# Whole products for the first pair of gate and up blocks, and three pieces of down kept behind the last block product

## The chip, the cores and the metric

The kernel runs on one core of a Trainium2 chip. The metric is the device time of one execution in microseconds (us). The core's engines work side by side, each through its own queue in order: TensorE (PE, matrix products), VectorE (DVE), ScalarE (ACT), GpSimd (POOL) and SyncE (SP, which issues most DMAs). They wait for one another by semaphores.

## What is computed

Two blocks in float32, one after the other. The first has two layers of attention. The second puts 16 meta tokens ahead of 512 rows, and goes through an even mixer, a convolutional feed-forward, an odd mixer, a second feed-forward and a last norm. The change lies in the two feed-forwards:

```python
def conv_ffn(h, w_up, w_gate, conv_w, conv_b, w_down):
    u = h @ w_up
    g = h @ w_gate
    g = lax.conv_general_dilated(g, conv_w[:, None, :].astype(g.dtype), window_strides=(1,),
                                 padding=[(CONV_WIDTH - 1, 0)],
                                 dimension_numbers=('NWC', 'WIO', 'NWC'),
                                 feature_group_count=D_FF) + conv_b
    return (jax.nn.silu(g) * u) @ w_down
...
        h = h + conv_ffn(rmsnorm(h, norm_ffn[l]), ffn_w_up[l], ffn_w_gate[l],
                         ffn_conv_w[l], ffn_conv_b[l], ffn_w_down[l])
    return rmsnorm(h, norm_final)[:, N_META:N_META + S]
```

The model is 1024 wide, the feed-forward 2816, the convolution 3 rows long.

## The kernel before

The residual X lies in SBUF transposed: 8 row blocks of 128 features, 528 columns of tokens (the second feed-forward uses 516 of them for gate and up and 512 for down). A float32 product is made of three products of rounded parts: each operand is split into a high part (ACT, a copy) and a low part (DVE, the difference), and the matmuls are high x high, high x low, low x high. `weights` (lines 149 to 165) loads a weight tile of 128 x 1024 by SP's queue into `wr` and splits it into `wh` and `wl`; `split` (lines 169 and 170) does the same for anything else; `dense` (line 179) issues matmuls.

A feed-forward has 22 blocks of 128 for gate and for up, taken in 11 pairs: i and i + 11. `paired` makes both blocks of a pair of one matrix by seven products of quarters in place of eight (lines 1204 to 1257): four sums of weight quarters (`ws`, line 1216), lows of 1024 columns of the raw weights (`wl`), of the sums (`wl`, `wx`) and one of 512 (`wy`), and then 7 products x 4 row blocks x 3 parts = 84 matmuls of 264 columns (258 in the second feed-forward; line 1240), in the banks `ps_a` and `ps_mm`. Copies by ACT (lines 1244, 1247, 1250) and sums by DVE (1251, 1256) put the result together. The right operands of the seven are made by `seven` (lines 1155 to 1202) from X and the norm's gain: the parts of two quarters (1172, 1173, 1182, 1183), sums of quarters t1 to t4 (1180, 1186 to 1188) and their splits, with the square sums of the norm (246, 249, 256) beside them. The norm's factor `rs` is taken into gate and up only behind the products; it comes by ones matmuls (256), ACT (226), POOL (227), transposes by PE (273) and an ACT copy (1201).

For each pair: gate, its product by rs (1136 to 1138), the convolution (1084 by ACT, two steps of 1086 by DVE), silu (1087, ACT), once more times rs (1088, POOL), up, the product of both (1142 to 1144), and a split into `aH` and `aL` (7 buffers each). The products by down are 8 pieces for each group of pairs (`after`; the groups are cut at 0, 1, 3, 5, 7, 9, 11): a piece adds one row block of X (1113). `between` puts pieces of the group before into places between the products of a pair. In the first feed-forward the last group's pieces follow at the end; in the second, `final` does the last group by halves of columns together with the last norm (lines 1259 to 1284).

Ahead of each feed-forward a mixer ends with products by its output weights (yH and yL are its operands, line 179), and DVE adds each to X (line 708). The order of all instructions on each engine is set by the language's scheduler, which goes by its own costs and by the buffers that come free.

Of the kernel before, what the change touches and what calls it, by code (L numbers as in the profile page):

```python
# [9 lines left out]
F32 = mybir.dt.float32  # L10
F32R = mybir.dt.float32r
AF = mybir.ActivationFunctionType
# [18 lines left out]
def two(x):  # L31

    return x.rearrange("p (a b) -> p a b", a=2)
# [29 lines left out]
class Norm:  # L63
# [35 lines left out]
    def done(self):  # L99
        rs = self.net.row_tile("rs", self.w)  # L100
        for out, a, b in self.net.rstd(self.pp, self.sums, 1.0 / D):
            self.net.nc.scalar.activation(rs[:, a:b], out, AF.Copy)
        return self.h, rs


class Net:
# [958 lines left out]
    def ffn(self, l, out=None):  # L1065
# [6 lines left out]
        with ExitStack() as c:  # L1072
# [2 lines left out]
            new = lambda name, cols, bufs, dt=F32: fp.tile([128, cols], dt, name=name, tag=name, bufs=bufs)  # L1075
            cw = fp.tile([128, 22, 4], F32, name="cw")
            nc.gpsimd.dma_start(cw, d[f"conv_{l}"])
            ops, rs = self.seven(pp, fp, X, self.gain[:, 6 + l])
            act, units = ([], []), []

            def activated(i, g):
# [32 lines left out]

                return [lambda o=o: unit(o) for o in range(8)]

            slots = 0

            def between():

                nonlocal slots
                for _ in range(-(-len(units) // max(slots, 1))):
                    units.pop(0)()
                slots -= 1

            cuts = (0, 1, 3, 5, 7, 9, 11)
            for a, b in zip(cuts, cuts[1:]):
                slots = 4 * (b - a)
                for i in range(a, b):
                    g = [new("g", lead + n, 3) for _ in range(2)]  # L1130
                    if u == 0:
                        for t in g:
                            nc.vector.memset(t[:, :2], 0.0)
                    e = g[0][:, lead - u:]
                    f, t = self.paired(pp, fp, d[f"gate_{l}"], i, ops, e, m, between)
                    nc.vector.tensor_tensor(e, e, rs, op=OP.mult)  # L1136
# [9 lines left out]
                        done(t)  # L1146
                if out is None or b < 11:
                    units += after(a, b)
            if out is None:
                for unit in units:  # L1150
                    unit()
            else:
                self.final(pp, fp, d[f"down_{l}"], act, 2 * a, 2 * b, out)

    def seven(self, pp, fp, x, g):

        nc, w = self.nc, x.shape[2]
        m = w // 2  # L1160
        ng = fp.tile([128, 8], F32, name="ng")
        nc.vector.tensor_scalar(ng, g, -1.0, None, op0=OP.mult)
        free = [self.hp.tile([128, T2], F32R, name="h", tag="h", bufs=16)[:, :w] for _ in range(16)]
        more = lambda: free.pop() if free else fp.tile([128, T2], F32R, name="op", tag="op", bufs=12)[:, :w]
        first = [[more() for _ in range(2)] for _ in range(2)]
        sums = self.sums(pp, w, 8)
        ops = [([], []) for _ in range(4)]
        for k in range(4):
            j = k + 4
            x1, x2, gk, gj = x[:, k], x[:, j], g[:, k:k + 1], g[:, j:j + 1]  # L1170
            h, l = (first[i][k // 2][:, m * (k % 2):m * (k % 2) + m] for i in range(2))
            nc.scalar.activation(h, x1[:, :m], AF.Copy, scale=gk)
            nc.vector.scalar_tensor_tensor(l, x1[:, :m], gk, h.bitcast(F32), op0=OP.mult, op1=OP.subtract)
            ops[0][0].append(h)
            ops[0][1].append(l)
            b12 = fp.tile([128, T2], F32, name="z", tag="z", bufs=4)[:, :m]
            nc.scalar.activation(b12, x1[:, m:], AF.Copy, scale=gk)
            s = [fp.tile([128, T2], F32, name="g", tag="g", bufs=3)[:, :w] for _ in range(2)]
            t1, t2, t3, t4 = s[0][:, :m], s[0][:, m:], s[1][:, :m], s[1][:, m:]
            nc.vector.scalar_tensor_tensor(t1, x1[:, :m], gk, b12, op0=OP.mult, op1=OP.subtract)  # L1180
            h, l = more(), more()
            nc.scalar.activation(h, x2, AF.Copy, scale=gj)
            nc.vector.scalar_tensor_tensor(l, x2, gj, h.bitcast(F32), op0=OP.mult, op1=OP.subtract)
            ops[1][0].append(h)
            ops[1][1].append(l)
            nc.vector.scalar_tensor_tensor(t2, x2[:, m:], ng[:, j:j + 1], t1, op0=OP.mult, op1=OP.subtract)
            nc.vector.scalar_tensor_tensor(t3, x2[:, m:], gj, b12, op0=OP.mult, op1=OP.subtract)
            nc.vector.scalar_tensor_tensor(t4, x2[:, :m], ng[:, j:j + 1], t2, op0=OP.mult, op1=OP.subtract)
            for i in range(2):
                h, l = more(), more()  # L1190
                self.split(h, l, s[i])
                ops[2 + i][0].append(h)
                ops[2 + i][1].append(l)
            sums(x1)
            sums(x2)
        lo, hi = slice(0, m), slice(m, w)
        cols = lambda i, c: [[t[:, c] for t in part] for part in ops[i]]
        right = {1: ops[0], 2: cols(1, lo), 3: cols(1, hi), 5: cols(2, lo), 6: cols(2, hi), 7: cols(3, lo), 4: cols(3, hi)}
        rs = self.row_tile("rs", w)
        for out, a, b in self.rstd(pp, sums, 1.0 / D):  # L1200
            nc.scalar.activation(rs[:, a:b], out, AF.Copy)
        return right, rs

    def paired(self, pp, fp, src, i, right, e, m, between):

# [196 lines left out]
```

## Time and profile before

| | us |
|---|---|
| median of 3 runs (lowest, highest) | 2141.17 (2140.36, 2142.55) |
| the profiled execution | 2140.01 |
| its span in the trace | 2138.3 |
| PE, DVE, ACT, POOL busy | 2034.8, 1518.1, 980.4, 570.6 |

Busy time is the sum of an engine's instructions in the span. The timeline gives for each instruction its start, its length, engine, line, operation, output and inputs, and in brackets the idle time ahead of it with what ended that. Neighbouring instructions overlap in it, so the price of one in a row of many is the step from one start to the next. A window gives the busy time of each engine in a stretch, the clock granted to PE (1.00 is 2.4 GHz, 0.50 is 1.2 GHz) and the DMA traffic.

### The profile page before, as it was taken

How to read it: one execution, taken by the hardware profiler on the slowest of the kernel's cores; microseconds unless marked ns; L12 is line 12 of the kernel's file. 1: busy time of each engine (PE TensorE's matmuls, PEld its weight loads, DVE VectorE, ACT ScalarE, POOL GpSimd, SP SyncE). 2: the span in 40 equal slices, each digit the busy share in tenths (PEclk: the TensorE clock that was granted, in tenths of full speed). 3: DMA queues.
4: the chain of work that ended last, by engine and by line, in shares of the span. 5: the costliest groups of instructions: out<-in, count | busy, mean ns of one | idle time of the engine just before them, and what ended most of it. 6: DMA issues, size and time to landing. Idle time of an engine off the chain costs nothing. (4 is left out here: it accounts for less than half of the span.)

```text
span 2138.3 us, 36583 instructions
## 1 busy us (share of the span) xinstructions
PE 2034.8 (95%) x14384; PEld 1863.6 (87%) x14384; DVE 1518.1 (71%) x2506; ACT 980.4 (46%) x1783; POOL 570.6 (27%) x652
## 2 busy tenths in 40 slices
PE   8999999999989999999989999999989988999997
PEld 6788888788889889988979999999878988889997
DVE  5565756665676896555788888875645788988885
ACT  5455645455644322344445444444334454544444
POOL 2322223222235555363001101103435401011011
PEclk9999999999999999999989999999989989999998
DMA  6643224533224322442222333324333222233222
GB/s 198 185 108 102 65 91 134 163 103 101 64 72 120 89 89 89 125 135 67 95 69 89 99 99 99 99 90 130 92 89 106 71 95 89 90 104 100 92 85 64
DMA packets 81163, 216.53 MB, mean 101 GB/s; under 512 B 10872, under 2 KB 16528, under 8 KB 80992
## 3 DMA queue, kind: packets, MB, share of 16 engines
q1 hardware_dynamic: 77360, 205.93, 32.2%
q0 software_dynamic: 2336, 7.19, 1.2%
q8 instruction: 113, 1.85, 0.4%
q10 hardware_dynamic: 1296, 1.09, 0.2%
q14 instruction: 58, 0.48, 0.1%
HBM read 166.20 MB, written 6.92 MB: 81 GB/s over the span
## 5 line engine op out<-in xcount | busy, mean ns | idle before, releaser
L179 PE MATMUL ps_mm<-hH,wh 128*128 128x264 f32 (+3 forms) x1480 | 393.1, 322 | 18.4 <-ACT hH L82 6.9
L179 PE MATMUL ps_mm<-hL,wh 128*128 128x264 f32 (+3 forms) x1480 | 395.1, 320 | 11.4 <-DVE hL L83 11.4
L179 PE MATMUL ps_mm<-hH,wl 128*128 128x264 f32 (+3 forms) x1480 | 393.6, 319 | 0.0
L163 ACT ACTIVATE wh<-wr 128x1024 fp32r<-128x1024 f32 (+3 forms) x213 | 209.4, 984 | 266.4 <-PE ps_mm L179 204.0
L179 PEld LDWEIGHTS ps_mm<-hH,wh 128*128 128x128 f32 (+1 forms) x1480 | 249.4, 191 | 38.6 <-DVE t L203 7.8
L164 DVE TENSOR_TENSOR wl<-wr,wh 128x1024 fp32r<-128x1024 f32 (+3 forms) x189 | 230.8, 1222 | 66.6 <-ACT wh L163 61.6
L179 PEld LDWEIGHTS ps_mm<-hL,wh 128*128 128x128 f32 (+1 forms) x1480 | 250.7, 191 | 29.4 <-DVE hL L83 13.0
L179 PEld LDWEIGHTS ps_mm<-hH,wl 128*128 128x128 f32 (+1 forms) x1480 | 250.8, 191 | 18.0 <-issue 1.4
L1088 POOL TENSOR_TENSOR z<-z,rs 128x528 f32<-128x528 f32 (+1 forms) x44 | 82.9, 1900 | 591.4 <-ACT z L1087 591.4
L179 PE MATMUL ps_mm<-aH,wh 128*128 128x264 f32 (+2 forms) x528 | 139.5, 319 | 6.3 <-ACT aH L169 4.1
L179 PE MATMUL ps_mm<-aL,wh 128*128 128x264 f32 (+2 forms) x528 | 138.6, 317 | 0.8 <-DVE aL L170 0.8
L179 PE MATMUL ps_mm<-aH,wl 128*128 128x264 f32 (+2 forms) x528 | 135.3, 316 | 0.1
L203 DVE TENSOR_TENSOR t<-ps_mm,rs 128x528 f32<-128x528 f32 (+1 forms) x101 | 70.2, 696 | 88.6 <-PE ps_mm L179 83.1
L1240 PE MATMUL ps_a<-h,wh 128*128 128x264 f32 (+1 forms) x528 | 103.1, 288 | 9.3 <-DVE z L1143 4.5
L169 ACT ACTIVATE wh<-ws 128x1024 fp32r<-128x1024 f32 x44 | 46.6, 1059 | 126.3 <-PE ps_mm L179 80.0
L179 PEld LDWEIGHTS ps_mm<-aH,wh 128*128 128x128 f32 x528 | 88.9, 190 | 12.6 <-ACT aH L169 4.3
L179 PE MATMUL ps_mm<-yH,wh 128*128 128x264 f32 (+2 forms) x392 | 95.8, 310 | 0.2 <-DVE X L708 0.2
L179 PE MATMUL ps_mm<-yH,wl 128*128 128x264 f32 (+2 forms) x392 | 95.3, 309 | 0.0
L1240 PEld LDWEIGHTS ps_a<-h,wh 128*128 128x128 f32 x528 | 84.4, 192 | 12.5 <-issue 4.7
L179 PEld LDWEIGHTS ps_mm<-aL,wh 128*128 128x128 f32 x528 | 88.9, 190 | 7.2 <-DVE aL L170 1.7
L179 PE MATMUL ps_mm<-yL,wh 128*128 128x264 f32 (+2 forms) x392 | 94.1, 306 | 0.0
L179 PEld LDWEIGHTS ps_mm<-aH,wl 128*128 128x128 f32 x528 | 88.2, 190 | 5.8 <-DVE wl L164 0.3
(342 smaller groups left out, 5013.9 us busy)
## 6 DMA issues: line engine op xcount, KB each, us to landing
wr<-w1c SPq DMA_DIRECT2D x52, 512.0 KB, 3.9
wr<-gate SPq DMA_DIRECT2D x44, 512.0 KB, 3.2
wr<-up SPq DMA_DIRECT2D x44, 512.0 KB, 3.3
wr<-down SPq DMA_DIRECT2D x40, 512.0 KB, 3.6
ks<-st SPq DMA_DIRECT2D x48, 264.0 KB, 5.0
wr<-we_b SPq DMA_DIRECT2D x24, 512.0 KB, 3.6
wr<-wo_c SPq DMA_DIRECT2D x24, 512.0 KB, 3.8
qs<-st SPq DMA_DIRECT2D x64, 132.0 KB, 3.0
```

The lines of the kernel that those rows point to most:

```text
L163: nc.scalar.activation(high, raw, AF.Copy)
L164: getattr(nc, eng).tensor_tensor(low, raw, high.bitcast(F32), op=OP.subtract)
L169: self.nc.scalar.activation(high, x, AF.Copy)
L179: self.nc.tensor.matmul(p[:a.shape[2]], a[:, k], b[k][:, t], start=bool(first and k == 0 and j == 0), stop=bool(last and k == len(ah) - 1 ...
L203: self.nc.vector.tensor_tensor(f(out), v, f(r), op=OP.mult)
L1088: nc.gpsimd.tensor_tensor(z, z, rs[:, u:], op=OP.mult)
L1240: nc.tensor.matmul(ps, p[:, k], q[k], start=start and k == 0 and v == 0, stop=k == 3 and v == 2, skip_group_check=not start)
```

## The change

Pair 0 of gate and of up is done by whole products: `whole` takes both blocks of the pair through all 8 row blocks, 2 blocks x 8 x 3 parts x 2 halves of columns = 96 matmuls. Their right operands (`plain`) are the parts of X by halves; one quarter that the seven don't need (`b12`) is split into buffers of `aH` and `aL`. The norm and the sums of quarters for the seven now stand behind gate's whole products in the code; the sums use two `ws` buffers in place of three `g`. The loop over pairs begins at 1. In the last group `spare` is 3: three pieces of down aren't put between the products but follow the loop, in the second feed-forward ahead of `final`. The removed body of `seven` stands above.

```diff
--- before.py
+++ after.py
@@ -1075,7 +1075,19 @@
             new = lambda name, cols, bufs, dt=F32: fp.tile([128, cols], dt, name=name, tag=name, bufs=bufs)
             cw = fp.tile([128, 22, 4], F32, name="cw")
             nc.gpsimd.dma_start(cw, d[f"conv_{l}"])
-            ops, rs = self.seven(pp, fp, X, self.gain[:, 6 + l])
+            plain, norm, seven = self.operands(pp, fp, new, X, self.gain[:, 6 + l])
+
+            def whole(src):
+
+                banks = [self.bank(pp, 0, w) for _ in range(2)]
+                W = [self.weights(src[11 * j]) for j in range(2)]
+                for k in range(8):
+                    for (wh, wl), (_, ps, _) in zip(W, banks):
+                        for j, (p, part) in enumerate(((wh, 0), (wh, 1), (wl, 0))):
+                            for h in range(2):
+                                nc.tensor.matmul(ps[h][0], p[:, k], plain[h][part][k], start=k == 0 and j == 0, stop=k == 7 and j == 2)
+                return [v for _, _, v in banks]
+
             act, units = ([], []), []
 
             def activated(i, g):
@@ -1114,23 +1126,44 @@
 
                 return [lambda o=o: unit(o) for o in range(8)]
 
-            slots = 0
+            spare, slots = 0, 0
 
             def between():
 
                 nonlocal slots
-                for _ in range(-(-len(units) // max(slots, 1))):
+                for _ in range(-(-max(len(units) - spare, 0) // max(slots, 1))):
                     units.pop(0)()
                 slots -= 1
 
-            cuts = (0, 1, 3, 5, 7, 9, 11)
+            def gates():
+                g = [new("g", lead + n, 3) for _ in range(2)]
+                if u == 0:
+                    for t in g:
+                        nc.vector.memset(t[:, :2], 0.0)
+                return g
+
+            v = whole(d[f"gate_{l}"])
+            rs = norm()
+            ops = seven()
+            g = gates()
+            for j in range(2):
+                nc.vector.tensor_tensor(two(g[j][:, lead - u:]), v[j], two(rs), op=OP.mult)
+            z = [activated(11 * j, g[j]) for j in range(2)]
+            v = whole(d[f"up_{l}"])
+            for j in range(2):
+                if u == 0:
+                    nc.vector.tensor_tensor(two(z[j]), two(z[j]), v[j], op=OP.mult)
+                else:
+                    nc.vector.tensor_tensor(z[j][:, m - u:], z[j][:, m - u:], v[j][:, 1], op=OP.mult)
+                    nc.vector.tensor_tensor(z[j][:, :m - u], z[j][:, :m - u], v[j][:, 0, u:], op=OP.mult)
+                done(z[j])
+            units += after(0, 1)
+
+            cuts = (1, 3, 5, 7, 9, 11)
             for a, b in zip(cuts, cuts[1:]):
-                slots = 4 * (b - a)
+                slots, spare = 4 * (b - a), 3 if b == 11 else 0
                 for i in range(a, b):
-                    g = [new("g", lead + n, 3) for _ in range(2)]
-                    if u == 0:
-                        for t in g:
-                            nc.vector.memset(t[:, :2], 0.0)
+                    g = gates()
                     e = g[0][:, lead - u:]
                     f, t = self.paired(pp, fp, d[f"gate_{l}"], i, ops, e, m, between)
                     nc.vector.tensor_tensor(e, e, rs, op=OP.mult)
@@ -1146,13 +1179,13 @@
                         done(t)
                 if out is None or b < 11:
                     units += after(a, b)
-            if out is None:
-                for unit in units:
-                    unit()
-            else:
+            for unit in units:
+                unit()
+            if out is not None:
                 self.final(pp, fp, d[f"down_{l}"], act, 2 * a, 2 * b, out)
 
-    def seven(self, pp, fp, x, g):
+    def operands(self, pp, fp, new, x, g):
+
 
 
 
@@ -1165,41 +1198,54 @@
         first = [[more() for _ in range(2)] for _ in range(2)]
         sums = self.sums(pp, w, 8)
         ops = [([], []) for _ in range(4)]
+        b12 = [], []
+
+        def parts(h, l, x, gain):
+            nc.scalar.activation(h, x, AF.Copy, scale=gain)
+            nc.vector.scalar_tensor_tensor(l, x, gain, h.bitcast(F32), op0=OP.mult, op1=OP.subtract)
+            return h, l
+
         for k in range(4):
...
+            pair = tuple(first[i][k // 2][:, m * (k % 2):m * (k % 2) + m] for i in range(2))
+            for out, pair, t, j in ((ops[0], pair, x[:, k, :m], k), (b12, tuple(new(n, S if w < T2 else T2, 7, F32R)[:, :m] for n in ("aH", "aL")), x[:, k, m:], k)):
+                for i, v in enumerate(parts(*pair, t, g[:, j:j + 1])):
+                    out[i].append(v)
+            sums(x[:, k])
+        for k in range(4, 8):
+            for i, v in enumerate(parts(more(), more(), x[:, k], g[:, k:k + 1])):
+                ops[1][i].append(v)
+            sums(x[:, k])
         lo, hi = slice(0, m), slice(m, w)
         cols = lambda i, c: [[t[:, c] for t in part] for part in ops[i]]
-        right = {1: ops[0], 2: cols(1, lo), 3: cols(1, hi), 5: cols(2, lo), 6: cols(2, hi), 7: cols(3, lo), 4: cols(3, hi)}
...
+        join = lambda a, b: [p + q for p, q in zip(a, b)]
+        plain = join(ops[0], cols(1, lo)), join(b12, cols(1, hi))
+
+        def norm():
+            rs = self.row_tile("rs", w)
+            for out, a, b in self.rstd(pp, sums, 1.0 / D):
+                nc.scalar.activation(rs[:, a:b], out, AF.Copy)
+            return rs
+
+        def seven():
+            for k in range(4):
+                j = k + 4
+                x1, x2, gk, gj = x[:, k], x[:, j], g[:, k:k + 1], g[:, j:j + 1]
+                b = fp.tile([128, T2], F32, name="z", tag="z", bufs=4)[:, :m]
+                nc.scalar.activation(b, x1[:, m:], AF.Copy, scale=gk)
+                s = [fp.tile([128, 1024], F32, name="ws", tag="ws", bufs=2)[:, :w] for _ in range(2)]
+                t1, t2, t3, t4 = s[0][:, :m], s[0][:, m:], s[1][:, :m], s[1][:, m:]
+                nc.vector.scalar_tensor_tensor(t1, x1[:, :m], gk, b, op0=OP.mult, op1=OP.subtract)
+                nc.vector.scalar_tensor_tensor(t2, x2[:, m:], ng[:, j:j + 1], t1, op0=OP.mult, op1=OP.subtract)
+                nc.vector.scalar_tensor_tensor(t3, x2[:, m:], gj, b, op0=OP.mult, op1=OP.subtract)
+                nc.vector.scalar_tensor_tensor(t4, x2[:, :m], ng[:, j:j + 1], t2, op0=OP.mult, op1=OP.subtract)
+                for i in range(2):
+                    h, l = more(), more()
+                    self.split(h, l, s[i])
+                    ops[2 + i][0].append(h)
+                    ops[2 + i][1].append(l)
+            return {1: ops[0], 2: cols(1, lo), 3: cols(1, hi), 5: cols(2, lo), 6: cols(2, hi), 7: cols(3, lo), 4: cols(3, hi)}
+
+        return plain, norm, seven
```

PE at the start of the first feed-forward; the rows end with the norm's transposes. Before:

```order
L1240 MATMUL ps_mm<-op,wh 128x264 x2
L1240 MATMUL ps_mm<-op,wl 128x264
L256 MATMUL ps_n<-ones,accd 128x1
L256 MATMUL ps_n<-ones,accd 16x1
L256 MATMUL ps_n<-ones,accd 128x1 x3
L1240 MATMUL ps_a<-h,wx 128x264 x2
L273 MATMUL ps_n<-ident,rsm 128x128 x4
L273 MATMUL ps_n<-ident,rsm 128x16
L1240 MATMUL ps_mm<-op,wh 128x264 x2
```

And after, from the last matmuls of gate's whole products to the first of up's:

```order
L1088 MATMUL ps_mm<-h,wl 128x264 x2
L256 MATMUL ps_n<-ones,accd 128x1
L256 MATMUL ps_n<-ones,accd 16x1
L256 MATMUL ps_n<-ones,accd 128x1 x3
L1286 MATMUL ps_a<-h,wh 128x264 x2
L1286 MATMUL ps_a<-h,wl 128x264
...
L273 MATMUL ps_n<-ident,rsm 128x128 x4
L273 MATMUL ps_n<-ident,rsm 128x16
L1088 MATMUL ps_mm<-h,wh 128x264
L1088 MATMUL ps_mm<-aH,wh 128x264
```

The norm, which stood between products of pair 0, now stands between gate's and up's whole products, with 12 matmuls of pair 1 (8 rows, six of them left out) between the ones and the transposes.

DVE from the second-last addition of a mixer tile to X (line 708) to the first operations behind the last one, first feed-forward. Before:

```order
L708 TENSOR_TENSOR X<-X,ps_mm 128x528
L170 TENSOR_TENSOR wl<-wr,wh 128x1024
L1186 SCALAR_TENSOR_TENSOR g<-X,ng,g 128x264
L1183 SCALAR_TENSOR_TENSOR op<-X,gain,op 128x528
L249 TENSOR_TENSOR accd<-accd,sq 128x528
L1183 SCALAR_TENSOR_TENSOR h<-X,gain,h 128x528
L1216 TENSOR_TENSOR ws<-wr 128x512 x2
L708 TENSOR_TENSOR X<-X,ps_mm 128x528
L170 TENSOR_TENSOR wx<-ws,wx 128x1024
L170 TENSOR_TENSOR h<-g,h 128x528 x2
```

After:

```order
L708 TENSOR_TENSOR X<-X,ps_mm 128x528
L164 TENSOR_TENSOR wl<-wr,wh 128x1024
L1205 SCALAR_TENSOR_TENSOR h<-X,gain,h 128x528
L1205 SCALAR_TENSOR_TENSOR h<-X,gain,h 128x264
L708 TENSOR_TENSOR X<-X,ps_mm 128x528
L1205 SCALAR_TENSOR_TENSOR aL<-X,gain,aH 128x264
L249 TENSOR_TENSOR accd<-accd,sq 128x528
L164 TENSOR_TENSOR wl<-wr,wh 128x1024
L249 TENSOR_TENSOR accd<-accd,sq 128x528
L1205 SCALAR_TENSOR_TENSOR h<-X,gain,h 128x528
```

Weight sums and sums of quarters have moved from between the two X additions to behind them.

ACT at the end of the second feed-forward, from the copy of the last product (f) to the first square sum of `final`. Before:

```order
L1250 ACTIVATE f<-ps_a 128x258
L163 ACTIVATE wH<-wr 128x512 x3
L169 ACTIVATE aH<-z 128x512 x2
L163 ACTIVATE wH<-wr 128x512
L246 ACTIVATE accd<-X 128x256
```

After:

```order
L1296 ACTIVATE f<-ps_a 128x258
L163 ACTIVATE wH<-wr 128x512
L169 ACTIVATE aH<-z 128x512 x2
L163 ACTIVATE wH<-wr 128x512
L163 ACTIVATE wh<-wr 128x512
L246 ACTIVATE accd<-X 128x256
```

The two aH copies have moved ahead of the second and third weight copy.

## Rows read from the trace of the kernel before

**Rows 1.** The page, part 1: busy us, share of the span, instructions of each engine.

```profile
PE 2034.8 (95%) x14384; PEld 1863.6 (87%) x14384; DVE 1518.1 (71%) x2506; ACT 980.4 (46%) x1783; POOL 570.6 (27%) x652
```

**Rows 2.** Windows; columns: stretch, us, busy PE, PEld, DVE, ACT, POOL, clock, DMA share, GB/s.

```profile
1062.50:1120.00 57.50, 46.24 (x305) 42.30 (x304) 47.27 (x77) 27.79 (x46) 4.82 (x3) 0.88 0.17 56
1120.00:1180.00 60.00, 58.09 (x466) 56.85 (x465) 54.24 (x80) 29.40 (x43) 8.28 (x4) 1.00 0.29 97
1180.00:1300.00 120.00, 120.00 (x987) 120.00 (x986) 104.19 (x149) 56.60 (x84) 16.83 (x8) 1.00 0.31 100
1742.20:1800.00 57.80, 45.85 (x291) 41.22 (x290) 46.47 (x72) 27.06 (x45) 4.84 (x3) 0.88 0.18 58
```

**Rows 3.** Windows around the clock's slow stretches, columns as in rows 2.

```profile
1067.30:1074.10 6.80, 6.23 (x25) 5.62 (x26) 6.80 (x12) 1.64 (x3) 0.00 (x0) 0.50 0.00 0
1074.10:1077.50 3.40, 2.12 (x16) 1.78 (x16) 3.40 (x8) 2.48 (x4) 0.03 (x1) 1.00 0.05 13
1077.50:1084.30 6.80, 5.87 (x26) 5.18 (x26) 3.81 (x10) 2.47 (x6) 1.30 (x1) 0.50 0.22 71
2101.50:2108.30 6.80, 6.23 (x25) 5.64 (x26) 3.70 (x7) 2.98 (x7) 0.00 (x0) 0.50 0.01 5
```

**Rows 4.** Timeline of PE, start of the first feed-forward: start, us, instruction, count, idle ahead.

```profile
1061.99 0.41 PE L179 MATMUL ps_mm<-yL,wh 128*128 128x264 f32 x2
1062.23 0.41 PE L179 MATMUL ps_mm<-yH,wl 128*128 128x264 f32 x2
...
1067.59 0.81 PE L1240 MATMUL ps_mm<-h,wh 128*128 128x264 f32 x2 [1.28 <-DVE X L708]
...
1075.59 1.27 PE L256 MATMUL ps_n<-ones,accd 128*128 128x1 f32 x10 [0.87 <-DVE accd L249]
...
1078.85 1.33 PE L273 MATMUL ps_n<-ident,rsm 128*128 128x128 f32 x5 [0.93 <-POOL rsm L227]
```

**Rows 5.** Timeline of DVE, start of the first feed-forward; last row: block 1's sum.

```profile
1062.12 1.22 DVE L170 TENSOR_TENSOR wl<-wr,wh 128x1024 fp32r<-128x1024 f32 x1
1063.26 0.49 DVE L1186 SCALAR_TENSOR_TENSOR g<-X,ng,g 128x264 f32<-128x264 f32 x1
1063.66 0.77 DVE L1183 SCALAR_TENSOR_TENSOR op<-X,gain,op 128x528 fp32r<-128x528 f32 x1
1064.34 0.70 DVE L249 TENSOR_TENSOR accd<-accd,sq 128x528 f32<-128x528 f32 x1
1064.96 0.76 DVE L1183 SCALAR_TENSOR_TENSOR h<-X,gain,h 128x528 fp32r<-128x528 f32 x1
...
1066.84 0.70 DVE L708 TENSOR_TENSOR X<-X,ps_mm 128x528 f32<-128x528 f32 x1
...
1120.79 0.70 DVE L1256 TENSOR_TENSOR g<-g,ps_mm 128x528 f32<-128x528 f32 x1
```

**Rows 6.** Timeline of ACT: the copy of rs, end of the norm.

```profile
1080.22 0.67 ACT L1201 ACTIVATE rs<-ps_n 128x512 f32<-128x512 f32 x2 [1.03 <-PE ps_n L273]
```

**Rows 7.** Timelines of DVE and POOL: a low part beside the product by rs.

```profile
1130.73 2.27 DVE L170 TENSOR_TENSOR wl<-wr,wh 128x1024 fp32r<-128x1024 f32 x1
...
1129.51 4.68 POOL L1088 TENSOR_TENSOR z<-z,rs 128x528 f32<-128x528 f32 x2 [20.17 <-ACT z L1087]
```

**Rows 8.** Timeline of PE: end of the first feed-forward, start of the last stage.

```profile
1423.04 0.51 PE L179 MATMUL ps_mm<-aH,wh 128*128 128x264 f32 x2 [1.60 <-DVE u L1256]
...
2101.97 0.80 PE L179 MATMUL ps_mm<-aH,wh 128*128 128x256 f32 x2 [4.12 <-ACT aH L169]
```

**Rows 9.** Timelines of DVE and ACT, end of the second feed-forward: z x u, a weight copy, aH.

```profile
2099.29 0.68 DVE L1144 TENSOR_TENSOR z<-z,u 128x512 f32<-128x512 f32 x1
...
2100.77 0.63 ACT L163 ACTIVATE wH<-wr 128x512 fp32r<-128x512 f32 x1 [2.69 <-DMA wr<-down]
2101.31 1.13 ACT L169 ACTIVATE aH<-z 128x512 fp32r<-128x512 f32 x2
```

More of the change, by code (lines that the diff above doesn't have):

```diff
@@ L1167, in seven @@
         ops = [([], []) for _ in range(4)]
-        for k in range(4):
[L1169 to L1195, printed above, removed]
@@ L1196, in seven @@
+        for k in range(4, 8):
+            for i, v in enumerate(parts(more(), more(), x[:, k], g[:, k:k + 1])):
+                ops[1][i].append(v)
+            sums(x[:, k])
         lo, hi = slice(0, m), slice(m, w)
         cols = lambda i, c: [[t[:, c] for t in part] for part in ops[i]]
-        right = {1: ops[0], 2: cols(1, lo), 3: cols(1, hi), 5: cols(2, lo), 6: cols(2, hi), 7: cols(3, lo), 4: cols(3, hi)}
-        rs = self.row_tile("rs", w)
-        for out, a, b in self.rstd(pp, sums, 1.0 / D):
-            nc.scalar.activation(rs[:, a:b], out, AF.Copy)
@@ L1202, in seven @@
-        return right, rs
+        join = lambda a, b: [p + q for p, q in zip(a, b)]
[23 more added lines that the diff above has]
+            return {1: ops[0], 2: cols(1, lo), 3: cols(1, hi), 5: cols(2, lo), 6: cols(2, hi), 7: cols(3, lo), 4: cols(3, hi)}
```

## The prediction, made before the change was run

> **What bounds the kernel now.** I read the page first: TensorE (PE) is busy for 95% of the span, VectorE (DVE) for 71% [rows 1]. A kernel like this gains only where PE stands still or is slowed, so the windows came next. In the middle of the first feed-forward PE is busy for 120.00 of 120.00 us at full clock with 987 matmuls, 0.122 us each [rows 2]; two successive pairs of the timeline start 0.24 us apart, which is the same price [rows 4], and I use 0.1225. Nothing can be won there. At the start of the feed-forward it is otherwise: 117.5 us hold 305 + 466 matmuls, of which 15 are the small ones of the norm [rows 2, 4]. 756 x 0.1225 = 92.6 us, so 24.9 us are lost (22.0 of them in the first window). The second feed-forward's start reads alike: 45.85 us busy of 57.80 at clock 0.88, against 46.24 of 57.50 at 0.88 [rows 2]. I take 24.9 for both.
>
> The timeline says who is late. PE waits 1.28 us for the last mixer tile's addition to X (DVE, old line 708), 0.87 for a square sum (DVE), 0.93 for POOL in the norm [rows 4]. PE finished that tile at about 1062.4, DVE adds it at 1066.84 [rows 4, 5]: 4.4 us late, because weight lows and operand work stand ahead. DVE is busy in 4 of 5 us of this window, PE is not [rows 2]. The clock follows: two stretches of 6.8 us at 0.50, that is 1.2 GHz, the first behind these waits, the second behind 3.4 us in which PE was busy for 2.12 [rows 3]. At 6.23 and 5.87 us busy they cost half of that, 3.1 and 2.9.
>
> **The start of each feed-forward.** Removed: 2 x 84 matmuls by seven products; added: 2 x 96 whole ones. 24 x 0.1225 = 2.9 us more PE work per feed-forward, certain. DVE loses per feed-forward, at the steps from one start to the next in [rows 5] (1.14 for 1024 columns, 0.62 for 528, 0.40 for 264; 0.60 for 512 is an estimate from the 0.62): two 1024-wide and two 512-wide lows, eight sums of weights, ten combinations (six of them 264 wide, four 528), and gains four 264-wide lows and four 528-wide products: about -2.3 -1.2 -4.8 -4.9 +1.6 +2.5 = -9.1 us.
>
> *The first 11.8 us.* By the order the 96 matmuls of gate (line 1088) stand right behind the mixer's last product and want only the parts of X and weights. Between DVE's last two additions to X stand now a 1024-wide low and two part lows, 1.14 + 0.68 + 0.40, where a 1024-wide and a 264-wide one, two 528-wide ones, a square sum and two weight sums stood; the last X add comes at about 1063, as the first five of eight row blocks don't need it. Lost: 0, at most the 4.4 of before.
>
> *The norm.* It moves behind gate's products, to 1062.4 + 11.8 = 1074.2. Its square sums are there: DVE has by then 7.8 us of work behind the X add that starts at about 1063. From the ones to the copy of rs it took 1075.59 to 1080.89, 5.3 us [rows 4, 6]; up's bank waits for that copy. Behind the ones stand 12 matmuls of block 1, 1.5 us: 3.8 us lost, until 1079.5. Is there a slow stretch behind it? The nearest row is the same norm before: 3.4 us with 2.12 busy, and clock 0.50 after it [rows 3]; against that a wait of 1.60 alone at the feed-forward's end, whose next two matmuls took 0.51 us [rows 8], where two at half rate took 0.81 [rows 4]. I take the slow stretch: 3.1 us (0 at the least, 3.4 at the most).
> Here the Trainium skill, "TensorE: Matmul & The Clock Gate", section "What's actually happening", bears: the throttled state is the default and activity releases it. The trace agrees ([rows 3]); by the page as by the row a start without waits could stay at 2.4 GHz, and the sum would then be 3.1 us shorter for each feed-forward.
>
> *Block 1's first products.* From the last X add to the low part of block 1's second left operand (line 170, wl from ws), the order has on DVE 20 operations of 512 or 528 columns, five scalar_tensor_tensor of 528, thirteen of 264 and three of 1024: 20 x 0.62 + 5 x 0.68 + 13 x 0.40 + 3 x 1.14 = 24.4 us. DVE reaches the products by rs after 13.4 of them, at 1076.3, and waits for rs until 1079.5; the other 11.0 end at 1090.5. Up's 96 end at 1079.5 + 11.8 = 1091.3, or 1094.4 at the slow stretch. So this operand is just in time. POOL's product by rs lies in that place: beside it a 1024-wide low took 2.27 instead of 1.22 us [rows 5, 7], 1.05 more, hidden by the slow stretch and costing about 0.3 without it.
> The Trainium skill, "GPSIMD Engine Reference", section "Specifications", says why: its SBUF interface is shared with VectorE and collides with instructions that have two SBUF inputs. By the rule both POOL products would stretch what they meet, 2 x 1.05 us, and the sum would be up to 1.8 us longer without the slow stretch; the row shows it for one low of two.
> Behind up's end DVE has 2 products z x v (1.24), a 1024-wide low (1.14) and 10.6 us of lows, sums and X adds before f (line 1297), which product 3 waits for: about 13 us. PE has 60 matmuls of the block and 24 to 36 of down ready: 10.3 to 11.8 us. Lost 1.5 (0 to 2.7).
>
> *After that* the pipeline settles as before: 60 - 466 x 0.1225 = 2.9 us [rows 2], kept. Sum: 24.9 - (3.8 + 3.1 + 1.5 + 2.9) - 2.9 = 10.7 us won per feed-forward, 21.4 in all. Without the slow stretch 13.5 (with 0.3 for POOL), without the 1.5 too 15; with all bounds bad (4.4, 3.4, 2.7) 4.8.
>
> **Three pieces of down held back.** In the first feed-forward the wait of 1.60 us for the sum of u [rows 8] stays: the piece behind it needs the bank that this sum frees. 0. In the second the last product is followed by six matmuls and a wait of 4.12 us for aH [rows 8], then 6.8 us at 0.50 [rows 3], 3.1. aH was late twice over: z x u came at 2099.29, and ACT started aH only at 2101.31, behind a wH that had waited 2.69 for its DMA [rows 9]. Now aH stands ahead of the second and third wH, and only one of the three pieces (12 matmuls of 512 columns, by columns an estimate of 24 x 0.1225 = 2.9 us) really lands behind the last product; it waits for the sum of u, as in the 1.60 row. 4.12 + 3.1 = 7.2 us could go; back come that wait of 1.60 and, at the first matmuls of the last stage, waits on weights whose loads, lows and X adds now stand behind one another: 1.0 (if one step of [rows 9] shows) to 4.1 (if the old wait comes back whole). I take 3.1, near their middle as no row is nearer. 7.2 - 1.6 - 3.1 = 2.5, with 1.5 to 4.6 from these ends; a new slow stretch would take 3.1 off, -1.6.
>
> **Sum.** Profiled execution 2140.0 - 21.4 - 2.5 = 2116.1; the median of the runs is 1.2 above it: 2117.3, taken as 2117. Own range: 2111 (no slow stretch) to 2124 (nothing at the tail, and 2 us more lost at each start, of the 5.9 that the bad bounds allow), 57%.
>
> **Rivals.**
> *DVE stays the bound.* The start then shortens only by DVE's smaller work, less the added PE work where both stand in a row: 9.1 - 2.9 = 6.2 each, 12.4 + 2.5, time 2126.3 (2124 to 2132). For it: DVE is busy for 47.27 of 57.50 and still 54.24 of the next 60.00 us [rows 2]. Against: PE gets 192 x 0.1225 = 23.5 us of work that needs little of DVE. 21%.
> *Larger gain.* Norm without a slow stretch, block 1 without a wait, tail at 4.6: 15 x 2 + 4.6, time 2106.6, and below if the settling goes too. 6%.
> *Nothing moves, or the held pieces and the whole products only swap waits.* DVE's work is 9.1 us less but the four rounds of seven now come late through two ws buffers: 2141. 5%.
> *Slower.* Each round of seven goes ACT, DVE, ACT, DVE over two ws buffers shared with block 1's weight sums. If these rounds stand in a row behind rs, block 1's sum in gate (line 1302) comes no earlier than its 1120.79 before [rows 5], nothing is won, and 2 x 2.9 us of PE work stay: 2147. It decides if block 1's second left operand is not there by about 1112 (1120.8 less 72 matmuls); my walk has it at 1090.5, so DVE would have to wait 21 us more than I count. A tail at -1.6 alone doesn't do it. 11%.
>
> **Chances.** Forecast 57, DVE 21, larger 6, none 5, slower 11. The range 2105 to 2132 leaves out half of the larger gain and the last two cases, 19 in 100. Some 0.2% (4.3 us) is what a measurement of this kernel tells from no change. Faster 0.84, same 0.05, slower 0.11.
>
> **What would show it.** Right: L1088 following L179 without a wait, one wait at L273 and one at the first L1088 behind it, PEclk 1.00 from 1062 to 1074 and one stretch near 0.50 behind the norm; block 1's L1286 at about 1095; in the last stage a wait under 2 us for u and no 4 us wait for aH. Wrong: waits of PE for DVE's X or h in the first 12 us (then the walk on DVE is wrong); L1286 waiting for op or wl for more than 5 us (the DVE rival); waits behind L1302 past 1120 (slower); the last stage starting no earlier (no gain of the tail).

## The result, and the profile after

| | before | after |
|---|---|---|
| median, us (lowest, highest) | 2140.36 (2136.28, 2142.55) | 2107.24 (2105.43, 2112.95) |
| runs | 6 | 6 |
| profiled execution, its span, us | 2140.01, 2138.3 | 2108.12, 2106.4 |

The ratio is 0.985 with a 95% interval of 0.9836 to 0.9865: 33 us (1.5%) less, clear of no change, where 24 us were forecast. The range 2105 to 2132 holds the time near its lower end; the forecast's own range, 2111 to 2124, does not.

Part 1 of the page of after answers to [rows 1]: PE has 48 matmuls more and 11.7 us less busy time, as less of it runs at half clock.

```profile
PE 2023.1 (96%) x14432; PEld 1856.2 (88%) x14432; DVE 1502.7 (71%) x2480; ACT 973.8 (46%) x1771; POOL 568.2 (27%) x652
```

The windows of after, columns as in [rows 2]: the first feed-forward's start in two stretches, then the stretches behind the norm of both feed-forwards, where the prediction had put the clock at 0.50.

```profile
1062.50:1120.00 57.50, 54.95 (x445) 53.82 (x444) 55.79 (x86) 35.12 (x52) 5.59 (x4) 1.00 0.25 83
1120.00:1180.00 60.00, 56.91 (x452) 55.26 (x452) 52.34 (x74) 26.89 (x41) 6.38 (x4) 1.00 0.29 97
...
1081.50:1088.50 7.00, 6.93 (x57) 6.93 (x58) 6.95 (x14) 4.82 (x8) 0.00 (x0) 1.00 0.01 2
1744.30:1751.30 7.00, 6.90 (x57) 6.91 (x58) 6.92 (x13) 5.13 (x9) 0.00 (x0) 1.00 0.01 2
```

The first window holds 445 matmuls where 305 stood in [rows 2], at 1.00 and not 0.88. With the second, 445 + 452 less 15 small ones are 882 x 0.1225 = 108.0 of 117.5 us: 9.5 us lost, where it was 24.9.

PE's timeline of after, the places of [rows 4]: gate's whole products follow the mixer's last product without a wait, 12 matmuls stand between the ones and the transposes, up's begin 0.76 us late, and pair 1 waits 1.27.

```profile
1065.05 0.41 PE L179 MATMUL ps_mm<-yH,wl 128*128 128x264 f32 x2
1065.29 0.29 PE L1088 MATMUL ps_mm<-h,wh 128*128 128x264 f32 x1
...
1076.94 1.17 PE L256 MATMUL ps_n<-ones,accd 128*128 128x1 f32 x10
...
1080.01 0.80 PE L273 MATMUL ps_n<-ident,rsm 128*128 128x128 f32 x5
1081.57 0.39 PE L1088 MATMUL ps_mm<-h,wh 128*128 128x264 f32 x1 [0.76 <-ACT rs L1226]
...
1095.03 0.51 PE L1286 MATMUL ps_a<-h,wx 128*128 128x264 f32 x2 [1.27 <-ACT wx L169]
```

**Where the 31.9 us of the two spans came from.** The same instruction stands in both traces, and the difference of its starts tells what was won up to there. Four X and u sums on DVE, first of before, then of after: an addition ahead of the first feed-forward's start, the last of its down, one in the odd mixer, and in the second feed-forward the sum of u of the ninth pair, with two pairs still to come.

```profile
1038.39 0.70 DVE L708 TENSOR_TENSOR X<-X,ps_mm 128x528 f32<-128x528 f32 x1 [1.48 <-PE ps_mm L179]
...
1443.88 0.70 DVE L1113 TENSOR_TENSOR X<-X,ps_mm 128x528 f32<-128x528 f32 x1 [0.58 <-PE ps_mm L179]
...
1708.69 0.69 DVE L708 TENSOR_TENSOR X<-X,ps_mm 128x516 f32<-128x516 f32 x1 [2.05 <-PE ps_mm L179]
...
2037.69 0.68 DVE L1256 TENSOR_TENSOR u<-u,ps_mm 128x516 f32<-128x516 f32 x1
```

```profile
1041.92 0.70 DVE L708 TENSOR_TENSOR X<-X,ps_mm 128x528 f32<-128x528 f32 x1 [1.10 <-PE ps_mm L179]
...
1435.36 0.70 DVE L1125 TENSOR_TENSOR X<-X,ps_mm 128x528 f32<-128x528 f32 x1 [0.45 <-PE ps_mm L179]
...
1696.12 0.69 DVE L708 TENSOR_TENSOR X<-X,ps_mm 128x516 f32<-128x516 f32 x1 [2.02 <-PE ps_mm L179]
...
2010.81 0.68 DVE L1302 TENSOR_TENSOR u<-u,ps_mm 128x516 f32<-128x516 f32 x1
```

Ahead of the change after is 3.53 us late; then it wins 12.05 in the first feed-forward, 4.05 in the mixer between, 14.31 in the second feed-forward up to its last two pairs, and 5.0 from there to the end, which is called the tail below. The first and third of these five lie in code whose order is the same in both kernels. The third goes with PE's waits in the odd mixer (line 1048) and the clock behind them: two waits for the DMA of ks took 2.96 and 3.41 us in before, each followed by a clock near half, and 1.17 and 1.42 in after, followed by 1.00; after has a wait of 2.96 with a slow stretch behind it further on, where before waits 0.93. Two windows of before behind its waits:

```profile
1555.50:1562.50 7.00, 6.83 (x30) 6.59 (x30) 0.17 (x1) 2.00 (x4) 0.00 (x0) 0.52 0.23 77
1590.40:1597.40 7.00, 6.96 (x31) 6.36 (x33) 0.17 (x1) 2.00 (x4) 0.00 (x0) 0.58 0.13 47
```

So the change itself won 12.05 + 14.31 + 5.02 = 31.4 us, and the other 0.5 is what is left of the two stretches of unchanged order. These vary: over the twelve kernels of the table below the first reads -1.2 to +4.4 us against before and the mixer -5.4 to +5.2, with nothing in it that follows the change. The same reckoning was made for each experiment; all numbers are differences to before, in us of the profiled execution:

| kernel | first feed-forward | second, to its last two pairs | tail | median |
|---|---|---|---|---|
| after | -12.05 | -14.31 | -5.02 | 2107.2 |
| after, again (e11) | -11.8 | -13.3 | -5.0 | 2106.2 |
| e1 no held pieces | -12.6 | -13.7 | -0.3 | 2112.5 |
| e2 held pieces alone | +2.2 | +0.9 | -5.2 | 2138.4 |
| e3 gate alone whole | -1.9 | -0.4 | -4.9 | 2134.1 |
| e10 e3 with g buffers | -5.1 | -8.4 | -4.8 | 2117.4 |
| e9 after with g buffers | -11.0 | -10.1 | -4.9 | 2112.1 |
| e5 longer norm | -10.7 | -12.8 | -5.1 | 2107.1 |
| e7 two pairs whole | -7.3 | -8.1 | -4.2 | 2121.1 |
| e6 rs on DVE | -13.0 | -14.5 | -4.9 | 2107.1 |
| e12 e6 again | -13.3 | -14.4 | -4.9 | 2104.0 |
| e13 e6, five pieces | -12.4 | -14.3 | -4.8 | 2107.5 |

Three profiles of the same start (after, e1, e11) differ by up to 1.0, and e2, whose start is that of before, by 2.2; I read differences under 1 us in this table only where a wait in the trace goes with them. The medians of before on the chips of the experiments were 2143.5 to 2146.1.

### The profile page after: what moved, and what is told of

It is laid out like the page before. It is cut to its first block, busy times and chain, and to the rows that moved or that the text cites. A ratio compares the mean times of both kernels' runs of the same rounds, so it can differ in the third digit from the quotient of the medians.

```text
span 2106.4 us, 36657 instructions
## 1 busy us (share of the span) xinstructions
PE 2023.1 (96%) x14432; PEld 1856.2 (88%) x14432; DVE 1502.7 (71%) x2480; ACT 973.8 (46%) x1771; POOL 568.2 (27%) x652
## 3 DMA queue, kind: packets, MB, share of 16 engines
q10 hardware_dynamic: 1296, 1.09, 0.2%
## 5 line engine op out<-in xcount | busy, mean ns | idle before, releaser
L179 PE MATMUL ps_mm<-hL,wh 128*128 128x264 f32 (+3 forms) x1480 | 395.6, 321 | 10.1 <-DVE hL L83 10.1
L163 ACT ACTIVATE wh<-wr 128x1024 fp32r<-128x1024 f32 (+3 forms) x221 | 217.8, 986 | 270.4 <-PE ps_mm L179 210.0
L164 DVE TENSOR_TENSOR wl<-wr,wh 128x1024 fp32r<-128x1024 f32 (+3 forms) x197 | 239.9, 1218 | 67.3 <-ACT wh L163 63.4
L179 PEld LDWEIGHTS ps_mm<-hL,wh 128*128 128x128 f32 (+1 forms) x1480 | 251.3, 192 | 28.1 <-DVE hL L83 11.7
L1286 PE MATMUL ps_a<-h,wh 128*128 128x264 f32 (+1 forms) x400 | 77.0, 285 | 4.4 <-DVE z L1176 4.3
L1286 PE MATMUL ps_mm<-h,wh 128*128 128x264 f32 (+1 forms) x400 | 76.0, 283 | 0.0
```

Source lines behind the costliest of these rows:

```text
L163: nc.scalar.activation(high, raw, AF.Copy)
L164: getattr(nc, eng).tensor_tensor(low, raw, high.bitcast(F32), op=OP.subtract)
L179: self.nc.tensor.matmul(p[:a.shape[2]], a[:, k], b[k][:, t], start=bool(first and k == 0 and j == 0), stop=bool(last and k == len(ah) - 1 ...
L1286: nc.tensor.matmul(ps, p[:, k], q[k], start=start and k == 0 and v == 0, stop=k == 3 and v == 2, skip_group_check=not start)
```

## The experiments

### The two parts, each alone (e1, e2)

```diff
-                slots, spare = 4 * (b - a), 3 if b == 11 else 0
+                slots, spare = 4 * (b - a), 0
```

> The changed kernel without held pieces (spare is 0 throughout); the whole products stay. In the two profiles the place behind the last gate block runs 26.9 us earlier than before in the middle of the second feed-forward and 31.9 us earlier at the end, so theory A puts 5.0 us on the held pieces: about 2112 us, the wait for aH back at about 4 us with a slow stretch behind it. Rival B, that the last stage gained only the 2.5 us of the prediction and the rest is the earlier start: about 2109.5. Rival C, that the held pieces do nothing: 2107.

Measured 2112.53 us (2109.23 to 2113.34), tail -0.3: theory A. PE's timeline at the end of e1 has the old wait back:

```profile
2075.15 0.80 PE L179 MATMUL ps_mm<-aH,wh 128*128 128x256 f32 x2 [4.16 <-ACT aH L169]
```

The other way round, before with `spare` and nothing else:

> The kernel before with nothing but the three held pieces. Theory A (parts add up): 2140.4 - 5.0 = 2135.4 us. Rival B: 2.5 us, 2138. Rival C (the pieces pay only with the new start): 2140. The start of both feed-forwards should read as before, with two slow stretches each.

Measured 2138.43 us, ratio to before 0.9976 (0.996 to 0.9992), some 5 us (before's median beside it was 2143.9, so 2138 does not speak for rival B); tail -5.2. Theory A holds both times: the held pieces are worth 5 us, with the new start or without it, and the parts add up.

### Is one whole matrix cover enough (e3), and what holds it up (e10)

```diff
-            v = whole(d[f"up_{l}"])
...
+            e = new("u", w, 2)
+            f, t = self.paired(pp, fp, d[f"up_{l}"], 0, ops, e, m, between)
```

> Only gate's first pair by whole products; up's first pair by the seven. Theory A, that the gain is PE work which covers DVE while it makes the seven's operands: the cover is 11.8 us and not 23.5, DVE has the low part of the second left operand some 11 us behind rs, so PE waits 5 to 9 us more in each feed-forward, less 1.5 for 12 matmuls: 2114 to 2122 us. Rival B, that moving the norm and the sums behind X's additions is the gain and one matrix is cover enough: 2 x 1.5 us less, 2104.

Measured 2134.13 us: nearly all of the start's gain is gone, more than theory A asked for. PE's timeline of e3 at the first product by the seven:

```profile
1083.73 0.81 PE L1285 MATMUL ps_mm<-h,wh 128*128 128x264 f32 x2 [6.32 <-ACT wh L169]
```

ACT's timeline at the copy that PE waits for:

```profile
1082.62 1.06 ACT L169 ACTIVATE wh<-ws 128x1024 fp32r<-128x1024 f32 x1 [2.02 <-DVE ws L1261]
```

The window behind that wait, columns as in [rows 2]:

```profile
1083.60:1090.40 6.80, 5.60 (x22) 4.99 (x23) 6.80 (x9) 4.44 (x6) 3.74 (x2) 0.50 0.49 152
```

PE waits for the high part of the weight sums, ACT for the sums, and DVE makes them only when the seven's rounds have left the two ws buffers. The mechanism of the rival that the prediction called slower is here, only in this kernel. e10 puts the sums of quarters back into the three g buffers:

```diff
-                s = [fp.tile([128, 1024], F32, name="ws", tag="ws", bufs=2)[:, :w] for _ in range(2)]
+                s = [fp.tile([128, T2 + 2 if w == T2 else S + 4], F32, name="g", tag="g", bufs=3)[:, :w] for _ in range(2)]
```

> Only gate's first pair by whole products, as in the run before, and the sums of quarters in the three g buffers. There PE waited 6.32 us for the high part of the weight sums, which stood behind the seven's rounds in the two ws buffers. Theory A, the two buffers are the cause: the wait falls to 1 or 2 us and the slow stretch behind it goes, 2134 - 2 x (4 to 8) = 2118 to 2126 us. Rival B, DVE's and ACT's work is the cause, whatever buffers it uses: 2131 to 2135.

Measured 2117.39 us (2111.01 to 2121.34), 17 us under e3. The wait of 6.32 is gone, so in e3 the buffers were the cause of most. The other half of theory A missed: e10 still has a slow stretch in each feed-forward, behind waits of 1.31 and 1.62 us in the first and of 1.25 and 1.92 in the second. Windows of e10:

```profile
1084.00:1088.00 4.00, 3.81 (x16) 3.33 (x17) 2.87 (x8) 3.04 (x8) 0.14 (x1) 0.50 0.00 0
1754.00:1758.00 4.00, 3.93 (x16) 3.48 (x17) 3.18 (x6) 3.43 (x8) 0.01 (x1) 0.50 0.00 0
```

What is left against after, 10 us, is not cover alone, since after also has the other buffers. The next kernel, e9, has both matrices whole and the g buffers: by the table its two starts win 21.1 us and e10's 13.5. So with these buffers the second whole matrix is worth 7.6 us, though it adds 2 x 1.5 us of matmuls.

### The same buffers in the changed kernel (e9)

The same edit to after:

> The changed kernel with the sums of quarters for the seven in the three g buffers, as in the kernel before, and not in the two ws buffers. Theory A, the ws buffers keep the weight sums of pair 1 behind the seven's last round: they start earlier and pair 1's wait (1.27 us in the first, 1.05 us in the second feed-forward) goes, 2104 to 2106. Rival B, DVE's work alone sets them: 2107, the waits as they are.

Measured 2112.12 us (2109.59 to 2118.57): neither theory. Pair 1's wait did go, but the norm got later. PE's timeline of e9, first feed-forward:

```profile
1074.53 1.27 PE L256 MATMUL ps_n<-ones,accd 128*128 128x1 f32 x10 [1.14 <-DVE accd L249]
...
1079.08 1.33 PE L273 MATMUL ps_n<-ident,rsm 128*128 128x128 f32 x5 [1.92 <-POOL rsm L227]
1081.16 0.59 PE L1088 MATMUL ps_mm<-h,wh 128*128 128x264 f32 x1 [0.76 <-ACT rs L1226]
```

The window behind it:

```profile
1081.00:1088.00 7.00, 6.84 (x43) 6.84 (x44) 6.39 (x14) 3.02 (x6) 0.00 (x0) 0.73 0.00 0
```

With free ws buffers the scheduler has three weight sums of pair 1 and 2 of the 12 matmuls ahead of the norm's ones. The norm waits 1.14 us for DVE's last square sum, 10 matmuls are left between ones and transposes, and the clock drops behind it (0.65 over 7.0 us in the second feed-forward). The norm also takes longer: POOL's power lies beside a weight sum and two lows on DVE. POOL's timelines of after and of e9, first feed-forward:

```profile
1078.51 1.45 POOL L227 TENSOR_TENSOR rsm<-rsm,mhalf 128x5 f32<-128x5 f32 x1 [37.13 <-ACT rsm L226]
...
1076.19 2.83 POOL L227 TENSOR_TENSOR rsm<-rsm,mhalf 128x5 f32<-128x5 f32 x1 [39.24 <-ACT rsm L226]
```

It took 2.83 us in both feed-forwards of e9. A low lies beside it in after too, so that DVE's work is the reason is likely but not shown. On the whole the order with two ws buffers, the norm first, is worth more here than pair 1's wait.

### The norm and the clock (e5)

Two products by one on POOL behind the power of the norm:

```diff
+        for _ in range(self.more):
+            nc.gpsimd.tensor_tensor(out, out, self.ones[:out.shape[0]].to_broadcast(list(out.shape)), op=OP.mult)
```

> The changed kernel with two more POOL products by one in the norm of each feed-forward, about 1.3 us each: the wait at the first of up's whole products grows from 0.76 to about 3.4 us. Theory A, the clock stays at 1.00 because PE was busy all through the 12 us ahead of the norm: 2.6 us more per feed-forward, less up to 1.3 that block 1's wait gives back: 2110 to 2112.5. Rival B, the wait decides and the slow stretch of the prediction comes with it (half clock for 6.8 us, 3.1 us): 2115 to 2118.5.

Measured 2107.09 us (2105.16 to 2118.17), which says nothing by itself; by the table the starts win 1.3 and 1.5 us less than in after. The two products took 1.09 us together and not 2.6, and PE got a wait of 1.15 and 1.11 us at the transposes. POOL's and PE's timelines of e5, first feed-forward:

```profile
1075.67 1.09 POOL L229 TENSOR_TENSOR rsm<-rsm,ones 128x5 f32<-128x5 f32 x2
...
1076.82 0.81 PE L275 MATMUL ps_n<-ident,rsm 128*128 128x128 f32 x5 [1.15 <-POOL rsm L229]
```

The windows behind the norm, first and second feed-forward:

```profile
1078.30:1085.10 6.80, 6.72 (x43) 6.72 (x44) 6.74 (x12) 4.64 (x7) 0.00 (x0) 0.75 0.01 2
1741.00:1747.80 6.80, 6.71 (x55) 6.72 (x56) 6.73 (x13) 4.92 (x8) 0.00 (x0) 1.00 0.00 0
```

Nearly the same wait brought a drop in one feed-forward (the first 3.4 us of the window at 0.50, the rest at 1.00) and none in the other, so neither theory holds alone, and what decides between the two is not shown. The drop was half as long as the stretch that the prediction took, and cost less than it reads: 55 - 43 = 12 matmuls are 1.5 us, but pair 1's wait of 1.27 was not there behind it. From gate's first product to pair 2's sum of u, e5 takes 1.3 us more than after in the feed-forward with the drop and 1.1 in the one without.

### More whole pairs (e7)

`whole` for pairs 0 and 1, the loop from pair 2 on:

> The changed kernel with pairs 0 and 1 by whole products. 48 more matmuls, 5.9 us. Theory A, one pair is enough cover: left to win are the waits of some 2 us at pair 1 and part of the 3 us behind it in each feed-forward: 2107 + 5.9 - (4 to 8) = 2105 to 2109 us. Rival B, DVE is still what bounds the first 100 us and every whole pair pays: 2100. Rival C, nothing is left to win: 2113.

Measured 2121.13 us (2115.29 to 2126.85), worse than rival C and 14 us over the changed kernel. The table shows 11.8 of these, 11.0 at the two starts. 5.9 us are the matmuls. The rest, as far as the trace shows it, stands at the norm: no product of pair 1 by the seven is there to run between ones and transposes, PE waits 2.52 us, and the clock behind it is 0.74 (first) and 0.58 (second feed-forward). PE's timeline of e7, first feed-forward:

```profile
1077.96 1.33 PE L273 MATMUL ps_n<-ident,rsm 128*128 128x128 f32 x5 [2.52 <-POOL rsm L227]
```

The windows behind the norm in both:

```profile
1079.90:1086.90 7.00, 6.85 (x43) 6.85 (x44) 6.87 (x15) 5.56 (x10) 0.72 (x1) 0.74 0.15 53
1750.30:1757.10 6.80, 6.72 (x35) 6.72 (x36) 6.74 (x13) 5.39 (x9) 0.69 (x1) 0.58 0.17 59
```

### POOL beside DVE (e6, e11, e12)

In after three of the four weight sums of pair 1 lie beside POOL's products by rs: two take 2.43 us together and the third 1.81, where the fourth, behind POOL's end, takes 0.69. DVE's timeline of after:

```profile
1088.99 2.43 DVE L1262 TENSOR_TENSOR ws<-wr 128x512 f32<-128x512 f32 x2
1091.35 1.81 DVE L1262 TENSOR_TENSOR ws<-wr,ws 128x512 f32<-128x512 f32 x1
...
1093.19 0.69 DVE L1262 TENSOR_TENSOR ws<-wr,ws 128x512 f32<-128x512 f32 x1
```

POOL's timeline of after:

```profile
1089.18 3.42 POOL L1100 TENSOR_TENSOR z<-z,rs 128x528 f32<-128x528 f32 x2 [9.23 <-ACT z L1099]
```

The Trainium skill, "GPSIMD Engine Reference", section "Specifications", says that POOL shares its SBUF interface with VectorE and collides with instructions of two SBUF inputs; these sums are such. The trace agrees with it: 4.24 us for the three sums here, 1.97 in e6, where POOL's products are moved away.

```diff
-            z = [activated(11 * j, g[j]) for j in range(2)]
+            z = [activated(11 * j, g[j], nc.vector) for j in range(2)]
```

> The changed kernel with pair 0's two products by rs on DVE and not on POOL. In the changed kernel's trace the three weight sums beside POOL's products took 2.43 + 1.81 us where two took 1.29 and one 0.69 alone. Theory A, POOL's products stretch them: DVE gets 2.3 us back and gives 1.2 for the two products, so pair 1's wait of 1.27 us in the first feed-forward shrinks and the time is up to 1 us less for each feed-forward, 2105 to 2107; the weight sums read 0.6 each again. Rival B, the sums are slow for another reason: they stay at about 1.2 us each, and two products more on DVE cost 1.2 each, 2109.

The sums read 1.29 for two and 0.68 for the third, the two products 1.33 on DVE, and PE's wait at pair 1 is gone. DVE's timeline of e6:

```profile
1086.74 1.29 DVE L1262 TENSOR_TENSOR ws<-wr 128x512 f32<-128x512 f32 x2
1087.94 1.33 DVE L1100 TENSOR_TENSOR z<-z,rs 128x528 f32<-128x528 f32 x2
...
1089.19 0.68 DVE L1262 TENSOR_TENSOR ws<-wr,ws 128x512 f32<-128x512 f32 x1
```

The median, 2107.12 us, can't show a microsecond, so e12 repeats it beside the changed kernel (e11):

> The changed kernel once more, as the measure of the two runs beside it on the same chip: 2105 to 2110 us.

> Pair 0's products by rs on DVE, once more and beside the changed kernel. In the first trace each feed-forward's start was 0.9 us shorter than the changed kernel's by aligned instructions, while the median was the same. Theory A: 1.8 us less than the changed kernel beside it. Rival B: no difference over 1 us.

Control 2106.18 us (ratio to before 0.9819, 0.9803 to 0.9836), e12 2103.95 (0.9805, 0.9791 to 0.9818). 2.2 us is near the 1.8 of theory A, and by the table both starts are shorter by 1.1 to 1.5 us; but the intervals overlap, so the median alone does not settle it. From gate's first product to pair 2's sum of u the products on DVE win 0.8 to 1.6 us in all four feed-forwards (e6 against after, e12 against e11).

### More held pieces (e13)

e12 with `spare` 5 in place of 3:

> The run before with five held pieces in place of three. What is left in the changed kernel's tail is a wait of 0.92 us for the copy f ahead of the seventh product and 1.05 us for X in the last stage, and weight loads of 3 us on ACT's path. Theory A, three pieces cover the path already, and two more taken from between the products open it there: the wait for f grows by 1 to 2 us and the last stage starts no earlier, 1 to 2 us more than the run before. Rival B, the longer cover lets the last stage's weights arrive: 1 us less.

Measured 2107.48 us (ratio to before 0.9821, 0.9804 to 0.9838), 3.5 over e12, but the intervals overlap, and the table has only some 1 us between the two. The tail reads -4.8 where it was -4.9: two more pieces won nothing there. Theory A has that, but not its reason: the wait for f is gone and the one for X fell from 1.08 to 0.69 us, while PE meets a new wait of 1.10 us for a weight copy between the products. Three pieces are enough.

## Why the prediction was right, point by point

**What bounds the start.** Right: DVE was late, and work for PE that needs little of DVE was the remedy. With half of that work the starts win 13.5 us (e10) and not 21.1 (e9) with the g buffers, and 2.3 (e3) and not 26.4 (after) with the ws buffers; the second pair of numbers holds the buffers' wait as well. DVE's own work was to fall by 2 x 9.1 us and fell by 15.4 (1518.1 to 1502.7 busy). No run has the new order without whole products, so what the order and the smaller work on DVE give by themselves is not shown.

**The first 11.8 us.** Right: no wait, and the last X addition starts 0.8 us behind the mixer's products, where it was 4.4 before. DVE's timeline of after:

```profile
1066.06 0.70 DVE L708 TENSOR_TENSOR X<-X,ps_mm 128x528 f32<-128x528 f32 x1
```

**The norm.** 3.8 us were reckoned; from ones to up's first it took 4.63 us, with 1.5 us of work in it: 3.1.

**The slow stretch behind it.** This step failed. I took the nearest row, a stretch of 3.4 us with 2.12 busy and the clock at 0.50 behind it [rows 3], and put 3.1 us on each feed-forward. It did not come in the two profiles of the changed kernel (after, e11), nor in e1, e6, e12 and e13, which have the same norm: 1.00 behind all twelve. In the old stretch nothing stood between ones and transposes but two matmuls that waited themselves; here 12 ran there, and only 0.76 us stayed as a wait. The order showed these 12, and the sum had them as time but not as what they do for the clock. e7, with the same norm and none of them, fell to 0.74 and 0.58; that the 12 kept the clock up agrees with this, but e5 still had them and fell in one of two. e5, e7 and e9, which add 1 to 3 us of waits at this place, got a slow stretch in five of six feed-forwards: the term was real, and 1 us more of waits could bring it. Its size was wrong even then: in e5 the drop cost 1.5 us of matmuls and some 0.2 in the end, as pair 1 waits anyway.

**Pair 1.** 1.5 us were reckoned; the waits of the first feed-forward read 1.27 and under 0.5 twice, about 2. The effect of POOL's products was mis-sized: I gave one low part 1.05 us, and three sums paid 2.3. Without the slow stretch to hide it, that was the wait of 1.27, which is gone in e6. That L1286 reads 1095.03, as the prediction had it, is luck: its 1095 held the slow stretch, and the trace of after stands 2.8 us later here.

**Sum of the starts.** 10.7 each forecast, 12.05 and 14.31 measured (11.8 and 13.3 in e11); without the slow stretch the prediction had 13.5, and their mean is 13.2. That is in part luck: the norm cost less than reckoned and pair 1 more, and the prediction took one loss for both feed-forwards, where they differ by 2 us. It had read only the first of the second feed-forward's two windows, and why that one wins more is open.

**The tail.** 2.5 forecast, 5.0 measured. What goes was right: 7.2 us, the 4.12 and the stretch at 0.50. What comes back was mis-sized twice. PE's timeline of after, the start of z x u on DVE and of aH on ACT, and the window:

```profile
2068.70 0.29 PE L179 MATMUL ps_mm<-aH,wl 128*128 128x256 f32 x1
2069.06 0.50 PE L179 MATMUL ps_mm<-aH,wh 128*128 128x512 f32 x1
...
2074.60 0.38 PE L179 MATMUL ps_mm<-aH,wh 128*128 128x256 f32 x1 [1.05 <-DVE X L1318]
...
2069.52 0.68 DVE L1177 TENSOR_TENSOR z<-z,u 128x512 f32<-128x512 f32 x1
2070.24 1.15 ACT L169 ACTIVATE aH<-z 128x512 fp32r<-128x512 f32 x2 [1.44 <-DVE z L1177]
...
2065.00:2080.00 15.00, 13.75 (x99) 12.79 (x100) 11.01 (x22) 7.53 (x17) 0.00 (x0) 1.00 0.29 87
```

The held piece does not wait 1.6 us for the sum of u, since the six matmuls of the last stage go first: 0.2 us. And of the waits on loads, lows and X adds, for which I took 3.1 between 1.0 and 4.1, one of 1.05 is there, for an X add, the lower end. A wait of 0.36 us for a weight low between the products is new. So 1.6 us come back where 4.7 were reckoned, and 0.6 of the 7.2 stay open. ACT does start aH at 2070.24, 0.7 us behind the start of z x u at 2069.52, where it was 2.0 [rows 9].

**The first feed-forward's end.** The wait of 1.60 for u [rows 8] was to stay; it reads 0.80. Small, and not looked into.

**The rivals.** DVE as the bound (2126) did not come; the slower one (the seven's rounds late through two ws buffers) is not in the changed kernel, but e3 has it. The larger gain (2106.6, 6%) is nearest to what came, though by a tail of 5.0 and no slow stretch rather than by a pair 1 without a wait. So the mechanism held and two terms were mis-sized the same way, the slow stretch and what comes back at the tail; that the range still holds the time is due to its width, which the rivals gave it. Of the 9.8 us between 2117 and 2107.24, 5.0 are the starts, 2.5 the tail, 0.5 the unchanged mixers, and the rest is how the medians stand to the profiled executions (reckoned as 1.2 above, measured 0.9 below after's).

## What to carry to other kernels

Where a stage starts with an engine that must first make operands, give PE work that needs fewer of them, even if it is more matmuls: 48 more cost 5.9 us, and the two starts still got 26.4 us shorter. The amount has a best value here: half of it won 13.5 us with the better buffers for that kernel (e10), and twice of it (e7) lost 14 against the changed kernel, 5.9 of them its own matmuls. Buffers belong to the reckoning: the same two ws buffers cost e3 17 us and, in after, stood for 5 us less than the three g buffers (e9). And reckon a wait on PE together with what runs inside it: with 12 matmuls inside the clock behind the norm stayed at 1.00, without them (e7) it fell.

## What was not expected of the hardware

- The three 512-wide sums on DVE took 4.24 us beside POOL's products and 1.97 without them, more than the one row of before (2.27 for 1.22) had shown.
- A POOL power of 128 x 5 took 1.45 us, a product of the same shape 0.55. In e9, beside sums and lows on DVE, the same power took 2.83.
- Nearly the same wait at the same place (1.15 and 1.11 us) gave clock 0.75 in one feed-forward and 1.00 in the other (e5).
- Code of unchanged order differs by 3 to 5 us from before to other profiles, as much as one part of this change is worth; in the odd mixer this goes with PE's waits at line 1048 and the clock behind them.
